# Dilated attention of a hybrid decoder layer: score and value matmuls on the whole array, and one pool of 23 buffers

## The chip, the cores and the metric

The kernel runs on one core of a Trainium2 chip. The metric is the device time of one execution in microseconds (us), as a median over several runs. A core has a matrix engine (PE, with PEld for its weight loads), a vector engine (DVE), a scalar engine (ACT), a general engine (POOL) and a queue engine (SP) that starts most transfers. Each engine works through its own list of instructions in a fixed order and waits, through semaphores, for what its next instruction needs.

## The reference

One decoder layer, in float32, with 512 tokens of width 1024:

```python
y = hybrid_mixer(rms_norm(x, pre_mix_g), w_in, attn_gn_g, ret_gn_g, w_out);   x = x + rms_norm(y, post_mix_g)
y = memory_cross_attn(rms_norm(x, pre_mem_g), mem, ...);                      x = x + rms_norm(y, post_mem_g)
y = swiglu(rms_norm(x, pre_ffn_g), w_gate_up, w_down);                        x = x + rms_norm(y, post_ffn_g)
```

The mixer projects to an attention group (8 heads of 64) and a retention group (4 heads of 128), normalises both and projects the two together. The attention is the part that the change touches: three dilated windows, (128,1), (512,4) and (2048,16), merged by their softmax denominators. For 512 tokens this equals one causal softmax per head, in which a key that lies in several windows counts several times:

```python
outs = [window_attn_by_stride(q, k, v, w, r) for (w, r) in DILATED_PATTERNS]   # o, row max m, denominator l of each
m_all = max(m for _, m, _ in outs)
wts = [l * exp(m - m_all) for _, m, l in outs]
return sum(wt * o for wt, (o, _, _) in zip(wts, outs)) / sum(wts)
```

## The kernel before, in words

**Precision by splitting.** Most products run on the type `fp32r`, which the array takes in one pass. A float32 operand x is written as a high part (x rounded to `fp32r`, on ACT, line 90) and a low part (x minus the high part, on DVE, line 91); this is `split`. A product of two split operands is three matmuls, high by high, high by low and low by high (`mm3`, lines 84 to 86). Plain float32 matmuls are used in the retention, in the transposes and in the attention's values; the trace shows each such product as two records, each transpose as one.

**Weights.** All weights come in 67 chunks of 1 MB, 128 partitions by 2048 values. `load` (from line 101) takes a buffer `raw` for the transfer on SP's queue and a pair `wh`, `wl` for the split. `raw` comes from a pool `rawp` of its own with 2 buffers, the pair from the pool `up` of 20 buffers ("units" of 8 KB per partition), which holds nearly everything else that is large: activations, queries and keys, probabilities. A buffer is reused once its last reader is done.

**Who sets the order.** The program is written in an order that mixes the stages by hand (the attention heads are interleaved with `filler` units: the projections `mk` and `mv` of the memory's keys and values). A scheduler then sets each engine's own list; a change in one stage can therefore move instructions in another.

**The stages.** First comes the projection of the retention's queries and keys (`rqk`, 8 banks of results at a time) while x and the first weights arrive; then `rv`, `rg`, the retention with the attention's projections (`aq`, `ak`, `av`); the attention; the output projection (`o`), the cross attention (`q`, `xs`, `xo`, `o`), and the feed-forward part (`g`, `u`, `dn`).

**The attention, per head.** `att_scores` (from line 431) makes four blocks of scores. The left operand `qk[pr][:, ...]` holds a head's queries with the high part on one half of the partitions and the low part on the other; the right operand holds the keys' high part on both halves, so that the first matmul (line 443) makes qh·kh + ql·kh over 128 rows. The second (line 444) adds qh·kl over 64 rows only: `kl` holds the keys' low part on the head's own half. DVE adds the mask and takes the row maximum (`p`, line 448; then `anm`, line 450), ACT the exponential (line 453). `att_transposes` (from line 457) turns the 10 blocks of probabilities by PE into three banks `ptr`, and copies them out with two ACT copies and one DVE copy (lines 466 to 468) to the unit `pT`. `att_values` (from line 471) multiplies by the values in float32 (line 478): 64 columns of `av` for the left operand, the transposed probabilities as the right one, with the results of a pair of heads in the two halves of one bank `oT`, which ACT copies (line 482). `att_norm` (one per pair) then transposes `ot`, takes the norm in a chain of small DVE operations, and writes `ya`.

Of the kernel before, what the change touches and what calls it, by code (L numbers as in the profile page):

```python
# [11 lines left out]
F32 = mybir.dt.float32  # L12
F32R = mybir.dt.float32r
# [6 lines left out]
P = 128  # L20
D = 1024
# [17 lines left out]
def hybrid_layer(ctx, tc, t, out):  # L39
    nc = tc.nc  # L40
    cp = ctx.enter_context(tc.tile_pool(name="cp", bufs=1))
    up = ctx.enter_context(tc.tile_pool(name="up", bufs=20))
    rawp = ctx.enter_context(tc.tile_pool(name="rawp", bufs=2))
# [6 lines left out]
    def uname(p):  # L50
        cnt[0] += 1
        return f"{p}{cnt[0]}"
# [251 lines left out]
    off = [0, 512, 1024, 896]  # L304
# [64 lines left out]
    qk = [unit("qk", F32R) for _ in range(4)]  # L369
    kl = unit("kl", F32R)  # L370
    av = unit("av")
# [45 lines left out]

    def evict_av(b, ps):
        nc.scalar.mul(av[:, b * 512:(b + 1) * 512], ps, rstd0[:, b:b + 1])

# [7 lines left out]
    def att_scores(h):  # L428
        pr, hh = h // 2, h % 2
        rows = slice(hh * 64, hh * 64 + 64)  # L430
# [7 lines left out]
        for qb in (3, 2, 0, 1):  # L438
            n = (qb + 1) * P
            nn = max(n, 256)  # L440
            c = qk[pr][:, hh * S + qb * P:hh * S + (qb + 1) * P]
            ps = bk[sbank[qb][0]][:, sbank[qb][1]:sbank[qb][1] + nn]
            nc.tensor.matmul(ps, lhsT=c, rhs=qk[pr][:, (2 + hh) * S:(2 + hh) * S + nn], start=True, stop=False)
            nc.tensor.matmul(ps, lhsT=c[rows], rhs=kl[rows, pr * S:pr * S + nn], start=False, stop=True)
# [11 lines left out]

    def att_transposes(h):
        pt = pts.pop(h)
        u = unit("pT")
        bk = [bank("ptr") for _ in range(3)]  # L460
        for kb in (0, 1, 3, 2):
            ps = bk[off[kb] // 512]
            for qb in range(kb, TB):
                o = off[kb] % 512 + (qb - kb) * P
                nc.tensor.transpose(ps[:, o:o + P], pt[:, poff[qb] + kb * P:poff[qb] + (kb + 1) * P], ident)
        nc.scalar.copy(u[:, 0:512], bk[0])
        nc.vector.tensor_copy(u[:, 512:1024], bk[1])
        nc.scalar.copy(u[:, 1024:1280], bk[2][:, :256])
        pTs[h] = u

    def att_values(h):
        pr, hh = h // 2, h % 2
        rows = slice(hh * 64, hh * 64 + 64)
        if hh == 0:
            oTb[pr] = bank("oT")
        u = pTs.pop(h)
        for kb in range(TB):
            nc.tensor.matmul(oTb[pr][rows, kb * P:S], lhsT=av[:, kb * 512 + h * AD:kb * 512 + (h + 1) * AD],
                             rhs=u[:, off[kb]:off[kb] + S - kb * P], start=kb == 0, stop=kb == TB - 1)
        if hh == 1:  # L480
            ot = work("ot")
            nc.scalar.copy(ot, oTb.pop(pr))
            oTb[pr] = ot
# [27 lines left out]
    mem = {}  # L511

    def mem_prepare():
        raw = rawp.tile([P, KT, NM], F32, tag="raw", name=uname("memTr"))
        nc.sync.dma_start(raw, t["memT"])
        m = pair("memT")
        for k in range(KT):
            split(raw[:, k, :], *part(m, k * NM, NM), gT[:, 1, k:k + 1])
        mem["T"] = m
        mem["k"], mem["v"] = pair("kT"), pair("vm")  # L520

    def mem_stats():
        mrow = rawp.tile([P, 2, D], F32, tag="raw", name=uname("mrow"))
# [450 lines left out]
```

## Time and profile before

| what | value |
|---|---|
| median of 3 runs | 829.76 us (829.33 to 831.52) |
| span of the profiled execution, first to last instruction | 828.5 us |
| PE busy | 807.9 us (98%), 4108 matmul records |
| DVE, ACT, POOL busy | 396.6, 305.4, 132.8 us |
| read from memory | 83.11 MB |
| mean granted PE clock | 0.991 |

The profile gives the profiled execution its span but no separate time. The median of the runs is 1.3 us above that span.

How to read it: the page lists busy time by engine; the view of waits says which engine stood idle before which instruction, and for whom; the windows give busy time and PE's granted clock for chosen stretches; the timeline has a row for each instruction or run of equal ones, with its start, its duration and the idle time before it. Matmuls are pipelined, so their durations overlap: the price of one is the distance from its start to the next one's start, not its duration.

### The profile page before, as it was taken

To read this page: it belongs to the slowest core of one execution; us is meant where nothing else is said; L and a number is where in the kernel's file an instruction comes from. 1 tells how busy PE (TensorE), PEld (TensorE's weight loads), DVE (VectorE), ACT (ScalarE), POOL (GpSimd) and SP (SyncE) were. 2 spreads that over 40 slices of the span, in tenths; PEclk is the share of its full clock that TensorE was granted. 3 is DMA by queue.
4 is the path that set the end of the run, shared out by engine and by line. 5 is a ranking of instruction groups with operands and counts; after the bars stand their busy time and mean duration, and the time that the engine had idled before them with its cause. 6 is when DMAs were issued, how large, how long until landed. Compare 5 with 4: busy or idle time off the path is not lost. (4 is left out here: it accounts for less than half of the span.)

```text
span 828.5 us, 10220 instructions
## 1 busy us (share of the span) xinstructions
PE 807.9 (98%) x4108; PEld 675.7 (82%) x4108; DVE 396.6 (48%) x766; ACT 305.4 (37%) x537; POOL 132.8 (16%) x176
## 2 busy tenths in 40 slices
PE   9979999999999999999999899999999999999996
PEld 7768888877777878999988788888888888888884
DVE  5595168764565657758446441405050314222144
ACT  5504333466464733445435232222130305332110
POOL 0161024410110100300036300000000004236000
PEclk9998999999999999999999999999999999999998
DMA  8726212221124440524002340505050322521011
GB/s 305 291 77 236 94 51 87 73 95 52 51 70 175 163 153 0 197 109 153 1 1 102 127 153 1 203 1 203 1 203 1 121 82 74 182 102 51 1 51 51
DMA packets 15519, 85.86 MB, mean 104 GB/s; under 512 B 1904, under 2 KB 1904, under 8 KB 6896
## 3 DMA queue, kind: packets, MB, share of 16 engines
q1 hardware_dynamic: 14752, 84.16, 27.7%
q10 hardware_dynamic: 720, 1.06, 0.3%
q8 instruction: 32, 0.52, 0.3%
q14 instruction: 15, 0.12, 0.0%
HBM read 83.11 MB, written 2.10 MB: 103 GB/s over the span
## 5 line engine op out<-in xcount | busy, mean ns | idle before, releaser
L91 DVE TENSOR_TENSOR wl<-raw,wh 128x1024 fp32r<-128x1024 f32 (+1 forms) x135 | 166.5, 1267 | 102.6 <-ACT wh L90 70.2
L90 ACT CAST wh<-raw 128x1024 fp32r<-128x1024 f32 (+1 forms) x135 | 133.8, 1042 | 95.3 <-DMA raw<-in_w_in 38.1
L820 DVE TENSOR_TENSOR af<-sg,u 128x512 f32<-128x512 f32 x22 | 15.1, 686 | 133.7 <-PE u L86 133.7
L846 POOL TENSOR_TENSOR al<-af,ah 128x512 fp32r<-128x512 f32 x22 | 34.6, 1605 | 257.5 <-ACT ah L845 243.3
L84 PE MATMUL g<-h3h,wh 128*128 128x512 f32 (+1 forms) x192 | 72.1, 375 | 0.0
L84 PE MATMUL u<-h3h,wh 128*128 128x512 f32 (+1 forms) x192 | 71.7, 373 | 0.0
L85 PE MATMUL g<-h3l,wh 128*128 128x512 f32 (+1 forms) x192 | 71.3, 371 | 0.0
L86 PE MATMUL g<-h3h,wl 128*128 128x512 f32 (+1 forms) x192 | 71.3, 371 | 0.0
L85 PE MATMUL u<-h3l,wh 128*128 128x512 f32 (+1 forms) x192 | 71.3, 371 | 0.0
L86 PE MATMUL u<-h3h,wl 128*128 128x512 f32 (+1 forms) x192 | 71.3, 371 | 0.0
L84 PE MATMUL dn<-wh,ah 128*128 128x512 f32 x176 | 68.5, 389 | 0.0
L85 PE MATMUL dn<-wl,ah 128*128 128x512 f32 x176 | 68.5, 389 | 0.0
L86 PE MATMUL dn<-wh,al 128*128 128x512 f32 x176 | 68.5, 389 | 0.0
L817 ACT ACTIVATE sg<-g 128x512 f32<-128x512 f32 x22 | 13.1, 598 | 149.2 <-PE g L86 123.0
L84 PEld LDWEIGHTS g<-h3h,wh 128*128 128x128 f32 x192 | 36.5, 190 | 6.5 <-ACT h3h L90 0.2
L84 PEld LDWEIGHTS u<-h3h,wh 128*128 128x128 f32 x192 | 36.6, 191 | 6.3
L85 PEld LDWEIGHTS g<-h3l,wh 128*128 128x128 f32 x192 | 36.2, 188 | 6.4
L86 PEld LDWEIGHTS g<-h3h,wl 128*128 128x128 f32 x192 | 36.2, 188 | 6.2
L85 PEld LDWEIGHTS u<-h3l,wh 128*128 128x128 f32 x192 | 36.2, 188 | 6.2
L86 PEld LDWEIGHTS u<-h3h,wl 128*128 128x128 f32 x192 | 36.1, 188 | 6.1
L84 PEld LDWEIGHTS dn<-wh,ah 128*128 128x128 f32 x176 | 33.0, 188 | 6.9
L86 PEld LDWEIGHTS dn<-wh,al 128*128 128x128 f32 x176 | 33.0, 188 | 6.9
(267 smaller groups left out, 1752.8 us busy)
## 6 DMA issues: line engine op xcount, KB each, us to landing
raw<-in_w_gu SPq DMA_DIRECT2D x22, 1024.0 KB, 4.8
raw<-in_w_in SPq DMA_DIRECT2D x12, 1024.0 KB, 5.1
raw<-in_w_dn SPq DMA_DIRECT2D x11, 1024.0 KB, 4.7
raw<-in_w_kv SPq DMA_DIRECT2D x8, 1024.0 KB, 4.7
x<-in_x SPq DMA_DIRECT2D x4, 1024.0 KB, 10.2
raw<-in_w_out SPq DMA_DIRECT2D x4, 1024.0 KB, 5.3
raw<-in_w_q SPq DMA_DIRECT2D x4, 1024.0 KB, 5.3
raw<-in_w_o SPq DMA_DIRECT2D x4, 1024.0 KB, 4.7
```

Of the source, the lines that this page charges most:

```text
L84: nc.tensor.matmul(o, lhsT=sh, rhs=mh, start=start, stop=False)
L85: nc.tensor.matmul(o, lhsT=sh, rhs=ml, start=False, stop=False)
L86: nc.tensor.matmul(o, lhsT=sl, rhs=mh, start=False, stop=stop)
L90: nc.scalar.copy(hi, src)
L91: nc.vector.tensor_sub(lo, src, hi.bitcast(F32))
L817: nc.scalar.activation(sg, pg, AF.Silu)
L820: nc.vector.tensor_mul(af[-1][:, (f % 4) * S:(f % 4 + 1) * S], sg, pu)
L846: nc.gpsimd.tensor_sub(lo[:, c], af[i][:, c], hi[:, c].bitcast(F32))
```

## The change

It has four parts.

1. **Scores.** `kl` is now two units. They hold the keys' low part on both halves of the partitions (8 more POOL copies of 64x512), so that the second score matmul uses all 128 rows of the left operand.
2. **Values.** `av` becomes two units of `fp32r`, in which each head's 128 columns are 64 high and 64 low ones (4 more DVE instructions). The transposed probabilities are split into a high and a low unit (`pair("pT")`; three ACT and three DVE instructions per head, where two ACT copies and one DVE copy stood), with two small POOL memsets of zeros. A head's values are 8 `fp32r` matmuls with 128 columns on the left; the upper 64 partitions of the bank hold the part of the high columns, the lower 64 that of the low ones. ACT copies the lower half out (`ol`) and DVE adds the upper half (`ot`), for each head.
3. **Buffers.** The pool `rawp` goes; `raw` comes from the pool `up`, which has 23 buffers in place of 20.
4. A scratch area for transfers is made smaller (`dynamic_dma_scratch_size=1024`).

```diff
-    up = ctx.enter_context(tc.tile_pool(name="up", bufs=20))
-    rawp = ctx.enter_context(tc.tile_pool(name="rawp", bufs=2))
+    up = ctx.enter_context(tc.tile_pool(name="up", bufs=23))
...
-        raw = rawp.tile([P, 2048], F32, tag="raw", name=uname("raw"))
+        raw = unit("raw")
...
-    kl = unit("kl", F32R)
-    av = unit("av")
+    kl = [unit("kl", F32R) for _ in range(2)]
+    av = [unit("av", F32R) for _ in range(2)]
...
+            l = kl[f // 2][:, (f % 2) * 2 * S + i * S:(f % 2) * 2 * S + (i + 1) * S]
             nc.scalar.copy(o[h], v[h])
-            nc.vector.tensor_sub(kl[h, f * S:(f + 1) * S], v[h], o[h].bitcast(F32))
+            nc.vector.tensor_sub(l[h], v[h], o[h].bitcast(F32))
             nc.scalar.copy(o[g], o[h].bitcast(F32))
+            nc.gpsimd.tensor_copy(l[g], l[h].bitcast(F32))
...
     def evict_av(b, ps):
-        nc.scalar.mul(av[:, b * 512:(b + 1) * 512], ps, rstd0[:, b:b + 1])
+        o = av_block(b).rearrange("p (h t d) -> p h t d", h=AH, t=2)
+        v = ps.rearrange("p (h d) -> p h d", h=AH)
+        nc.scalar.mul(o[:, :, 0, :], v, rstd0[:, b:b + 1])
+        nc.vector.scalar_tensor_tensor(o[:, :, 1, :], v, rstd0[:, b:b + 1], o[:, :, 0, :].bitcast(F32),
+                                       op0=ALU.mult, op1=ALU.subtract)
...
-            nc.tensor.matmul(ps, lhsT=c[rows], rhs=kl[rows, pr * S:pr * S + nn], start=False, stop=True)
+            nc.tensor.matmul(ps, lhsT=c, rhs=kl[pr // 2][:, k0:k0 + nn], start=False, stop=True)
...
+    pcol = [(0, 512, 0), (512, 384, P), (1152, 256, 2 * P), (896, 256, 2 * P)]
     def att_transposes(h):
...
-        nc.scalar.copy(u[:, 0:512], bk[0])
-        nc.vector.tensor_copy(u[:, 512:1024], bk[1])
-        nc.scalar.copy(u[:, 1024:1280], bk[2][:, :256])
+        for a in (hi, lo):
+            nc.gpsimd.memset(a[:, 896:1024].bitcast(F32), 0.0)
+        for i, (c0, n) in enumerate(((0, 512), (512, 384), (1024, 384))):
+            split(bk[i][:, :n], hi[:, c0:c0 + n], lo[:, c0:c0 + n])
...
     def att_values(h):
-        for kb in range(TB):
-            nc.tensor.matmul(oTb[pr][rows, kb * P:S], lhsT=av[:, kb * 512 + h * AD:kb * 512 + (h + 1) * AD],
-                             rhs=u[:, off[kb]:off[kb] + S - kb * P], start=kb == 0, stop=kb == TB - 1)
+        for kb, (c0, n, q0) in enumerate(pcol):
+            for i in range(2):
+                nc.tensor.matmul(ps[:, q0:q0 + n], lhsT=av_block(kb, h, 1), rhs=u[i][:, c0:c0 + n],
+                                 start=kb == 0 and i == 0, stop=kb == TB - 1 and i == 1)
...
+        ol = work("ol")
+        nc.scalar.copy(ol[ha], ps[hb])
+        nc.vector.tensor_add(oTb[pr][rows], ps[ha], ol[ha])
```

**How it moves instructions: PE in the attention.** Before, the rows on PE's list from the scores of head 5 to the values of head 3 (`s` scores, `oT` values, `p` probabilities) read:

```order
L443 MATMUL s_1836<-qk_685 128x512
L444 MATMUL s_1836<-kl_687,qk_685 128x512
L443 MATMUL s_1837<-qk_685 128x384
L444 MATMUL s_1837<-kl_687,qk_685 128x384
L443 MATMUL s_1838<-qk_685 128x256
L444 MATMUL s_1838<-kl_687,qk_685 128x256
L443 MATMUL s_1838<-qk_685 128x256
L444 MATMUL s_1838<-kl_687,qk_685 128x256
L478 MATMUL oT_1782<-pT_1787,av_688 64x512
L478 MATMUL oT_1782<-pT_1787,av_688 64x384
L478 MATMUL oT_1782<-pT_1787,av_688 64x256
L478 MATMUL oT_1782<-pT_1787,av_688 64x128
```

Now, after the same scores of head 5, PE's list has (`ptr` are the transposes of head 4):

```order
L490 MATMUL oT_1913<-pTh_1838,av_686 128x512
L475 MATMUL ptr_1927<-ident,p_1765 128x128 x4
L490 MATMUL oT_1913<-pTl_1839,av_686 128x512
L490 MATMUL oT_1913<-pTh_1838,av_686 128x384
L475 MATMUL ptr_1928<-ident,p_1765 128x128 x2
L490 MATMUL oT_1913<-pTl_1839,av_686 128x384
L490 MATMUL oT_1913<-pTh_1838,av_687 128x256
L475 MATMUL ptr_1928<-ident,p_1765 128x128
L475 MATMUL ptr_1929<-ident,p_1765 128x128
L490 MATMUL oT_1913<-pTl_1839,av_687 128x256
L490 MATMUL oT_1913<-pTh_1838,av_687 128x256
L490 MATMUL oT_1913<-pTl_1839,av_687 128x256
```

The values of head 3 are cut up and mixed with the next head's transposes, since each of the value matmuls needs its own piece of `pTl`.

**DVE at the same place.** Before, DVE's list around head 3's one copy (`pT_1787`) reads:

```order
L91 TENSOR_TENSOR wl_1747<-raw_1745,wh_1746 128x1024
L536 TENSOR_TENSOR kf_1778<-mk_1753,mbc 128x256
L467 COPY pT_1787<-ptr_1789 128x512
L536 TENSOR_TENSOR kf_1829<-mk_1804,mbc 128x256
L448 ISA p_1833,amx_1834<-s_1836,lmask 128x512
```

Now it reads:

```order
L496 TENSOR_TENSOR ot_1834<-oT_1825,ol_1835 64x512
L549 TENSOR_TENSOR kf_1886<-mk_1861,mbc 128x256
L90 TENSOR_TENSOR wl_1790<-raw_1788,wh_1789 128x1024 x2
L90 TENSOR_TENSOR pTl_1839<-ptr_1840,pTh_1838 128x512
L90 TENSOR_TENSOR pTl_1839<-ptr_1841,pTh_1838 128x384
L90 TENSOR_TENSOR pTl_1839<-ptr_1842,pTh_1838 128x384
L456 ISA p_1890,amx_1891<-s_1893,lmask 128x512
```

Head 3's low parts (`pTl_1839`), which its values wait for, now stand behind a result of the filler (`kf_1886`) and the split of a weight chunk (`wl_1790`).

**SP at the start.** Before, the transfers behind the last piece of x's transpose (`xraw`) are:

```order
L109 DMA raw_144<-in_w_in 128x2048
L109 DMA raw_156<-in_w_in 128x2048
L161 DMA x_152<-in_x 128x2x1024
L161 DMA x_153<-in_x 128x2x1024
L211 DMA rope_164<-in_rope 128x2048
```

Now they are:

```order
L283 DMA lmask<-in_lmask 128x512
L108 DMA raw_141<-in_w_in 128x2048
L167 DMA g_2349<-in_post_mix_g 128x1024
L167 DMA g_2565<-in_pre_mem_g 128x1024
L160 DMA x_149<-in_x 128x2x1024
L160 DMA x_150<-in_x 128x2x1024
L108 DMA raw_153<-in_w_in 128x2048
L210 DMA rope_161<-in_rope 128x2048
```

The fourth chunk of weights (`raw_156`, now `raw_153`) has moved behind 3.25 MB of other transfers, and on PE's list its first use has moved from the 103rd to the 126th matmul of this projection, while the broadcast of the row norms (`bc`, which DVE's chain of rotations waits for) has moved from the 121st to the 142nd.

**DVE ahead of the feed-forward part.** Before, between the last two normalised blocks `h`:

```order
L626 TENSOR_TENSOR z_4131<-o_4080,g_3470 128x512
L91 TENSOR_TENSOR wl_4190<-raw_4188,wh_4189 128x1024 x2
L91 TENSOR_TENSOR wl_4262<-raw_4260,wh_4261 128x1024 x2
L626 TENSOR_TENSOR z_4131<-o_4081,g_3470 128x512
L630 SCALAR_TENSOR_TENSOR x_2231<-z_4131,pry_4141,x_2231 128x512 x2
L635 SCALAR_TENSOR_TENSOR h_4170<-x_2231,nry_4159,g_3682 128x1024
```

Now:

```order
L639 TENSOR_TENSOR z_4246<-o_4195,g_3585 128x512
L90 TENSOR_TENSOR wl_4305<-raw_4303,wh_4304 128x1024 x2
L639 TENSOR_TENSOR z_4246<-o_4196,g_3585 128x512
L643 SCALAR_TENSOR_TENSOR x_2346<-z_4246,pry_4256,x_2346 128x512 x2
L648 SCALAR_TENSOR_TENSOR h_4285<-x_2346,nry_4274,g_3797 128x1024
```

One chunk's split, where two stood, is ahead of the last block; ACT's list loses the two casts of that chunk at the same place.

More of the change, by code (lines that the diff above doesn't have):

```diff
@@ L429, in att_scores @@
         pr, hh = h // 2, h % 2
-        rows = slice(hh * 64, hh * 64 + 64)
         if hh == 0:
@@ L473, in att_values @@
         rows = slice(hh * 64, hh * 64 + 64)
[L474 to L483 removed]
+        ps = bank("oT")
+        u = pTs.pop(h)
+        for kb, (c0, n, q0) in enumerate(pcol):
+            for i in range(2):
+                nc.tensor.matmul(ps[:, q0:q0 + n], lhsT=av_block(kb, h, 1), rhs=u[i][:, c0:c0 + n],
+                                 start=kb == 0 and i == 0, stop=kb == TB - 1 and i == 1)
+        if hh == 0:
+            oTb[pr] = work("ot")
+        ol = work("ol")
+        nc.scalar.copy(ol[ha], ps[hb])
+        nc.vector.tensor_add(oTb[pr][rows], ps[ha], ol[ha])
     def att_norm(pr):
@@ L513, in mem_prepare @@
     def mem_prepare():
-        raw = rawp.tile([P, KT, NM], F32, tag="raw", name=uname("memTr"))
+        raw = unit("memTr").rearrange("p (k s) -> p k s", k=KT)
         nc.sync.dma_start(raw, t["memT"])
@@ L522, in mem_stats @@
     def mem_stats():
-        mrow = rawp.tile([P, 2, D], F32, tag="raw", name=uname("mrow"))
+        mrow = unit("mrow").rearrange("p (b d) -> p b d", b=2)
         nc.sync.dma_start(mrow, t["mem"].rearrange("(b p) d -> p b d", p=P))
```

20 lines of the change are left out of this document (11 added, 9 removed).

## Prediction

> **What bounds the kernel now.** I read the page's busy times first, then PE's waits, then windows cut at these waits. A window's row gives its ends, its length, the busy time (and instructions) of PE, PEld, DVE, ACT and POOL, PE's granted clock, the DMA share and GB/s.
>
> ```profile
> PE 807.9 (98%) x4108; PEld 675.7 (82%) x4108; DVE 396.6 (48%) x766; ACT 305.4 (37%) x537; POOL 132.8 (16%) x176
> PE rv L85 <- DVE wl L91: 5.2, 1, 5.2
> PE tp L792 <- DVE h L635: 4.0, 1, 4.0
> 56.80:62.10 5.30, 0.14 (x2) 0.01 (x1) 5.18 (x8) 0.00 (x0) 3.58 (x3) 0.75 0.00 0
> 62.10:66.00 3.90, 3.90 (x9) 3.13 (x10) 3.90 (x3) 0.00 (x0) 1.06 (x1) 0.50 0.22 38
> 189.40:264.40 75.00, 74.91 (x422) 54.08 (x420) 44.75 (x133) 41.20 (x102) 6.56 (x8) 1.00 0.20 70
> 469.00:820.70 351.70, 351.61 (x1592) 293.05 (x1592) 104.09 (x129) 88.69 (x119) 34.64 (x22) 1.00 0.24 86
> 820.70:828.50 7.80, 0.00 (x0) 0.00 (x0) 3.81 (x12) 0.69 (x2) 0.00 (x0) 0.71 0.17 67
> ```
>
> PE is the bound nearly everywhere: of the span of 828.5 us it lacks work for two waits worth naming (5.2 and 4.0 us) and a tail of 7.8 us. The attention loop, from 189.4 to 264.4 us, is the stage that the change rewrites: PE is full there, with DVE at 44.75 and ACT at 41.20 of 75.0 us. A microsecond taken from PE there is a microsecond of the kernel, as long as DVE and ACT keep up.
>
> **Scores: what PE saves.** The timeline of PE gives one head's eight score matmuls between two runs of the filler:
>
> ```profile
> 237.97 0.28 PE L85 MATMUL mk<-memTl,wh 128*128 128x256 f32 x1
> 238.09 0.28 PE L86 MATMUL mk<-memTh,wl 128*128 128x256 f32 x1
> 240.01 0.39 PE L443 MATMUL s<-qk 128*128 128x512 f32 x1
> 240.33 0.50 PE L444 MATMUL s<-kl,qk 64*128 64x512 f32 x1
> 240.76 0.44 PE L443 MATMUL s<-qk 128*128 128x384 f32 x1
> 241.13 0.45 PE L444 MATMUL s<-kl,qk 64*128 64x384 f32 x1
> 241.50 0.38 PE L443 MATMUL s<-qk 128*128 128x256 f32 x1
> 242.76 0.39 PE L84 MATMUL mk<-memTh,wh 128*128 128x256 f32 x1
> 260.38 0.40 PE L86 MATMUL mv<-wh,memTl 128*128 128x512 f32 x1
> 260.61 0.39 PE L84 MATMUL mv<-wh,memTh 128*128 128x512 f32 x1
> ```
>
> Start to start, a full-array matmul of 256 columns costs 0.12 us and one of 512 costs 0.23; for 384 I take 0.175, halfway. In the scores the same sizes cost more: 512 columns 0.32 on all rows and 0.43 on 64 rows, 384 columns 0.37 and 0.37, and the head's eight take 240.01 to 242.76, 2.75 us. What sets them apart from the filler is the alternation of 128 and 64 rows, which ends with the change. The eight are then two of each: 2 x 0.23 + 2 x 0.175 + 4 x 0.12 = 1.29 us. Eight heads save 8 x 1.46 = 11.7 us. If the price lies not in the alternation but in these operands, nothing is saved: 0 is the lower bound. The Trainium skill, "TensorEngine Tiling (Array Packing)", section "Key Properties", says that changing the tiling mode drains the engine; by that rule every one of these gaps is a drain that goes, and the trace's gaps agree.
>
> **Values.** One head's float32 matmuls, eight records, from their start to the next instruction's:
>
> ```profile
> 262.06 2.37 PE L478 MATMUL oT<-pT,av 128*64 128x512 f32 x8
> 264.36 0.66 PE L300 MATMUL yt<-ident,rg 128*128 128x128 f32 x4
> ```
>
> That is 2.30 us. The new eight have 512, 384, 256 and 256 columns twice, so 1.29 us as above; eight heads save 8 x 1.01 = 8.1 us. If they ran at the scores' present spacing (2.64 us by the rows above), they would lose 2.7 us; I take the filler's, whose operands and array they share. PE saves 19.8 us in all, 6 x 1.46 + 8.1 = 16.9 of it inside the window of 75.0 us, which would shrink to 58.1.
>
> **What DVE and ACT pay there.** The groups by form in that window:
>
> ```profile
> L91 DVE TENSOR_TENSOR wl<-raw,wh 128x1024 fp32r<-128x1024 f32 x10 | 11.9, 1219 | 1.4 <-ACT wh L90 1.4
> L467 DVE COPY pT<-ptr 128x512 f32<-128x512 f32 x8 | 5.5, 688 | 8.6 <-PE ptr L465 8.6
> L536 DVE TENSOR_TENSOR kf<-mk,mbc 128x256 f32<-128x256 f32 x8 | 3.4, 424 | 12.1 <-PE mk L86 12.0
> L448 DVE CUSTOM_DVE_ANT_0 p<-s,lmask 128x512 f32<-128x512 f32 (+3 forms) x24 | 11.0, 488 | 2.8 <-PE s L444 2.7
> L503 DVE TENSOR_TENSOR ya<-otr,ary 128x512 f32<-128x512 f32 x3 | 2.1, 691 | 0.2
> L145 DVE TENSOR_TENSOR arw<-ary 128x8 f32<-128x8 f32 x9 | 1.5, 167 | 0.2
> L466 ACT COPY pT<-ptr 128x512 f32<-128x512 f32 x8 | 4.7, 584 | 11.7 <-PE ptr L465 11.6
> L468 ACT COPY pT<-ptr 128x256 f32<-128x256 f32 x8 | 3.0, 370 | 0.2
> 46.63 0.69 DVE L246 TENSOR_TENSOR t<-rqk,rope 64x512 f32<-64x512 f32 x1
> ```
>
> Per head DVE loses a copy (0.69) and gains three low parts, 1.79 us (0.69 for 512 columns and 0.55 for each of two with 384, halfway between the copy's 0.69 and `kf`'s 0.42 for 256), and the 64x512 addition (0.69, as the `t` row): +1.79 us. Eight heads: 14.3, so 44.75 becomes 59.1 us in a window that PE would leave after 58.1. ACT gains two casts of 384 for one copy of 256 (about 0.5 each against 0.37) and `ol` in each head for half an `ot` (0.59 against 0.29): +0.93 a head, 41.20 becomes 48.6, with room.
>
> So DVE catches up with PE, and the question is what PE waits. I went along both orders from head 2's transposes to head 6's values. PE: 62 transposes at 0.11 (the next rows), 4 scores and 5 values of 1.29, 7 fillers of 24 x 0.12: 38.6 us.
>
> ```profile
> 235.99 1.31 PE L465 MATMUL ptr<-ident,p 128*128 128x128 f32 x10
> 237.05 0.36 PE L84 MATMUL mk<-memTh,wh 128*128 128x256 f32 x1
> ```
>
> DVE: 5 x 1.79 of low parts, 5 x 0.69 of additions, 4 x 1.83 of `p` (11.0 us for six heads), 7 x 0.42 of `kf`, four chunks of `wl` (8 x 1.22), three norm chains of 3.6 (two large steps as `ya`, 13 small ones as `arw`) and four of `anm`, as small: 44 us. DVE falls 5.4 us behind. A little of that may be late without harm (the last norm, a chunk for later matmuls), and some is added where DVE itself stands waiting, for `kf_1886` above all, ahead of the low parts that head 3's values need. I take 5 us of waiting for PE. Bounds: 0 if the mixing of transposes with values hides it; 11.4 if DVE can be kept only 85% busy (59.1 / 0.85 - 58.1).
>
> **The rest.** The eight POOL copies for `kl`, the memsets and the four DVE instructions for `av` lie off PE's path. The copies run beside the projections of the keys, where PE has 24 x 0.23 = 5.5 us of work per step and a POOL operation of twice their size takes 1.46 us:
>
> ```profile
> L411 POOL TENSOR_TENSOR t<-t,rope 128x512 f32<-128x512 f32 x6 | 8.7, 1457 | 14.1 <-DVE t L409 14.0
> ```
>
> Without that cover the last four copies, 6 us at most, would hold up the scores of the later heads.
>
> At the start, the fourth weight chunk now follows 3.25 MB of other transfers, and the chain of rotations on DVE that ends PE's wait of 5.2 us begins later:
>
> ```profile
> 23.63 2.00 ACT L90 CAST wh<-raw 128x1024 fp32r<-128x1024 f32 x2 [1.64 <-DMA raw<-in_w_in]
> 35.84 2.00 ACT L90 CAST wh<-raw 128x1024 fp32r<-128x1024 f32 x2 [0.45 <-DMA raw<-in_w_in]
> 33.65 0.46 PE L176 MATMUL bc<-diag,ones 128*128 128x128 f32 x2 [0.30 <-DVE diag L175]
> 36.76 0.69 DVE L177 COPY rbc<-bc 128x512 f32<-128x512 f32 x1 [0.58 <-PE bc L176]
> ```
>
> Between 23.6 and 35.8 us five megabytes landed (x, `rope`, two chunks), so 3.25 MB cost about 8 us, and the chunk lands near 31 instead of 23.6. PE asked for it 18 matmuls ahead of the broadcast, near 29 us, and now asks 23 later, near 34: no stall. The broadcast stands 21 matmuls later, 0.23 each, so `rbc` and the end of PE's wait move by 4.4 to 4.8 us; but PE has 23 more matmuls (5.2 us) ahead of that wait. Net 0, from -1 to +4 if the transfers are slower.
>
> The second wait, ahead of the feed-forward part:
>
> ```profile
> 450.09 3.88 ACT L90 CAST wh<-raw 128x1024 fp32r<-128x1024 f32 x4
> 453.87 0.59 ACT L624 ACTIVATE junk<-o 128x512 bf16<-128x512 f32 x1
> 467.72 1.28 DVE L635 SCALAR_TENSOR_TENSOR h<-x,nry,g 128x1024 f32<-128x1024 f32 x1 [4.56 <-POOL nry L141]
> ```
>
> The squares of the last block stood behind four casts on ACT; one chunk's two casts (1.94 us) are gone from there, so the chain to `h` ends 1.9 us earlier. I take -2 us, between -4 (the wait gone) and 0.
>
> As all chunks now share the pool, most `raw` transfers wait for a unit that PE frees. Load and split take 4.7 + 2.1 + 2.4 = 9.2 us:
>
> ```profile
> raw<-in_w_kv SPq DMA_DIRECT2D x8, 1024.0 KB, 4.7
> ```
>
> By the order, with PE's matmuls priced as above, the tightest chunk of the attention (`raw_2288`) has its last unit freed 10 us of PE work before its first use, the others 12 or more: no cost, but little to spare.
>
> **Sum.** 828.5 - 19.8 + 5 + 0 - 2 = 811.7 us of span. The runs' median lies 1.3 us above the profiled span; with that, 813 us.
>
> **Rivals.**
>
> *DVE paces the attention.* If it is busy only 85% of the time, PE waits 11.4 us: 828.5 - 19.8 + 11.4 - 2 + 1.3 = 819.4. For it: its 59.1 us stand in a strict order with results of PE between them. Against: the waits of DVE today show idle time that is slack, not bubbles. It gets worse if PE's gaps grow long: after the wait of 5.2 us the clock row shows 0.50 for 3.9 us, 2 us lost; my gaps are 1 to 2 us each. The Trainium skill, "TensorE: Matmul & The Clock Gate", section "Why this matters for your kernels", puts the danger at idle gaps above about 3 us; one wait here (5.2 us) agrees, the other (4.0 us) was followed by the window from 469 us at clock 1.00.
>
> *The scores don't get cheaper.* If the spacing belongs to the operands, or if 64 rows were the cheap form, 11.7 us stay: with PE slower, DVE's lag goes too, 828.5 - 8.1 - 2 + 1.3 = 819.7; if the new values share that spacing it is 830.5. Against: 512 columns on 64 rows take 0.43 here, a full-array matmul 0.23. The Trainium skill speaks for it in "TensorEngine Tiling (Array Packing)", section "Theoretical Speedup": up to twofold for a contraction of 64 or less, when tiles run side by side; here each 64-row matmul stands between full ones, and its row bears no gain out.
>
> *Slower: the shared pool starves the weights.* A chunk whose unit PE frees less than 9.2 us before use stalls PE, and DVE's list stands still behind its `wl`. The kernel turns slower when such stalls pass 829.8 - 813 = 16.8 us; 1 us at each of the 33 feed-forward chunks gives 846, half of it on top of the first rival 836. Against: there each chunk has 48 x 0.23 = 10.9 us of PE work, and by the order its units are free 20 us or more ahead.
>
> **Chances.** Forecast 0.64 (808 to 817); DVE paces 0.18 (817 to 823); scores not cheaper 0.09 (820 to 831); starved and slower 0.05 (833 to 850); better than forecast, with no wait in the attention, 0.04 (805 to 808). The range 806 to 821 leaves out the starved case, nearly all of the third and the outer ends of the second and the last, 0.2 in all. A measurement of this kernel tells 0.3%, 2.5 us, from no change. Faster 0.93, the same 0.03, slower 0.04.
>
> **What would show it.** Right: the eight scores of a head span 1.3 us, the eight values 1.3 us of matmuls with gaps for `pTl` on DVE among PE's waits, 3 to 8 us in sum; DVE near full in the window; the wait on `h` at 2 us. Wrong: scores still at 0.3 us each; PE waiting for `wl` or `wh` with a transfer behind it; PE's clock below 1.00 in the attention.

## The result and the profile after

The changed kernel takes 840.08 us (median of 4 runs, 838.71 to 842.38) against 829.61 us before (4 runs): a ratio of 1.0126, 95% interval 1.0107 to 1.0145. It is slower by 10.5 us, where 813 us were forecast and 806 to 821 us given as the range. The profiled execution spans 836.9 us, 8.4 us more than before. One execution of e5 below, its profiled one, ran at half the matmul rate throughout (span 1597.0 us); it is left out, and that kernel was profiled again as e8.

The line of busy times on the page of the changed kernel:

```profile
PE 794.9 (95%) x4108; PEld 680.1 (81%) x4108; DVE 409.9 (49%) x794; ACT 310.4 (37%) x549; POOL 133.5 (16%) x200
```

and PE's longest waits in it (engine, line, what it waited for, us in total, times, longest):

```profile
PE rv L84 <- DVE wl L90: 5.7, 1, 5.7
PE q L85 <- DVE wl L90: 4.8, 4, 2.4
PE s L451 <- DVE av L426: 4.7, 1, 4.7
PE otr L503 <- DVE ot L496: 3.4, 2, 2.0
PE ptr L475 <- DVE pTl L90: 2.8, 1, 2.8
PE tp L805 <- DVE h L648: 2.6, 1, 2.6
PE mk L83 <- DVE ot L496: 1.7, 1, 1.7
PE q L83 <- ACT wh L89: 1.7, 1, 1.7
```

PE is busy 13 us less and yet ends later: two waits worth naming have become eight. Where the clock is full, a head's matmuls came down as forecast. The timeline of PE, one head's first score, first value and what follows:

```profile
207.85 0.40 PE L451 MATMUL s<-qk 128*128 128x512 f32 x1
...
209.14 0.40 PE L490 MATMUL oT<-pTh,av 128*128 128x512 f32 x1
...
210.43 1.25 PE L475 MATMUL ptr<-ident,p 128*128 128x128 f32 x10
```

Eight scores take 207.85 to 209.14, eight values 209.14 to 210.43: 1.29 us each, to the hundredth what the prediction worked out.

To see where the time went I cut both executions at the same PE instructions: the first scores, the first transposes of probabilities, the first `yt`, the first `q` and the first `xs` (windows as in the prediction: ends, length, busy PE, PEld, DVE, ACT, POOL, PE's clock). Before, from the first scores on, and the query projection:

```profile
172.35:189.46 17.11, 16.71 (x66) 11.76 (x64) 11.34 (x29) 11.94 (x25) 0.41 (x1) 1.00 0.19 62
189.46:264.36 74.90, 74.81 (x421) 54.04 (x419) 44.75 (x133) 41.14 (x102) 6.56 (x8) 1.00 0.20 70
331.50:357.37 25.87, 25.53 (x214) 25.29 (x213) 19.61 (x38) 11.65 (x24) 8.33 (x19) 1.00 0.57 204
```

The same three stages after:

```profile
174.78:195.51 20.73, 16.06 (x66) 13.09 (x64) 15.61 (x34) 14.38 (x28) 3.26 (x7) 0.84 0.15 51
195.51:263.63 68.12, 59.61 (x422) 55.85 (x421) 53.08 (x155) 44.94 (x112) 8.03 (x22) 0.97 0.31 109
332.64:366.32 33.68, 26.82 (x213) 25.57 (x212) 21.24 (x36) 13.98 (x26) 6.84 (x19) 1.00 0.34 126
```

The stage of the first two heads' scores was to lose 2 x 1.46 = 2.9 us and gained 3.6: 6.5 us are missing. The attention loop was to lose 6 x 1.46 + 8.1 = 16.9 and lost 6.8: 10.1 us missing. The query projection, in which the change edits nothing, gained 7.8. Up to the first scores the kernel is 2.4 us later, between loop and query projection 1.9, and behind it 0.5 are won back. In sum 6.5 + 10.1 + 7.8 + 2.4 + 1.9 - 0.5 = 28.2 us lost, less the 19.8 saved: 8.4.

In the query projection the transfers can be seen to come late. SP's timeline, the transfers of `w_q` and of the gain vectors; before:

```profile
292.92 41.89 SPq L109 DMA_DIRECT2D raw<-in_w_q  x4
...
344.25 0.33 SPq L168 DMA_DIRECT2D g<-in_post_mem_g  x1
```

and after:

```profile
291.76 22.02 SPq L108 DMA_DIRECT2D raw<-in_w_q  x2
340.18 0.33 SPq L167 DMA_DIRECT2D g<-in_post_mem_g  x1
340.60 0.38 SPq L108 DMA_DIRECT2D raw<-in_w_q  x1
348.46 0.33 SPq L167 DMA_DIRECT2D g<-in_pre_ffn_g  x1
348.84 0.43 SPq L108 DMA_DIRECT2D raw<-in_w_q  x1
```

What SP's queue waited longest for between 300 and 352 us in the changed kernel:

```profile
SPq L167 <- DVE z L639: 26.3, 1, 26.3
SPq L108 <- PE o L84: 21.3, 1, 21.3
```

Before, the four `w_q` transfers start at 292.9, 299.2, 331.9 and 334.5 us, the first two while the output projection still runs, into the two buffers that hold nothing but landing transfers. After, the second waits 21.3 us for a unit that PE's output projection holds, and the third and fourth stand in SP's order behind two gain vectors, of which the first waits 26.3 us for DVE's last `z`. PE asks for the first of these weights at 332.64. Which of this PE waits for, e6 below tells.

### The profile page after: what moved, and what is told of

It reads as the page before. It is cut to its first block, busy times and chain, and to the rows that moved or that the text cites. A ratio compares the mean times of both kernels' runs of the same rounds, so it can differ in the third digit from the quotient of the medians.

```text
span 836.9 us, 10294 instructions
## 1 busy us (share of the span) xinstructions
PE 794.9 (95%) x4108; PEld 680.1 (81%) x4108; DVE 409.9 (49%) x794; ACT 310.4 (37%) x549; POOL 133.5 (16%) x200
## 4 chain that ended last, share of the span: by engine, by line
PE 52%; DVE 4%; POOL 3%; issue 2%; DMA 1%; ACT 1%; DVEq 0%; SPq 0%; POOLq 0%; ACTq 0%
PE dn L84 5%; PE dn L83 5%; PE dn L85 5%; PE g L84 5%; PE g L85 5%; PE u L84 5%; PE u L85 5%; PE g L83 5%; PE u L83 4%; PE o L83 1%; PE o L85 1%; PE o L84 1%; PE q L85 1%; PE q L83 1%; PE q L84 1%
## 5 line engine op out<-in xcount | busy, mean ns | idle before, releaser
L90 DVE TENSOR_TENSOR wl<-raw,wh 128x1024 fp32r<-128x1024 f32 (+1 forms) x135 | 163.6, 1250 | 94.9 <-ACT wh L89 83.9
L859 POOL TENSOR_TENSOR al<-af,ah 128x512 fp32r<-128x512 f32 x22 | 31.2, 1452 | 255.3 <-ACT ah L858 248.8
L85 PE MATMUL q<-hhh,wl 128*128 128x256 f32 x128 | 35.9, 287 | 4.8 <-DVE wl L90 4.8
```

The costliest lines, as they stand in the source:

```text
L85: nc.tensor.matmul(o, lhsT=sl, rhs=mh, start=False, stop=stop)
L90: nc.vector.tensor_sub(lo, src, hi.bitcast(F32))
L859: nc.gpsimd.tensor_sub(lo[:, c], af[i][:, c], hi[:, c].bitcast(F32))
```

## Experiments

Two theories stood at the start. Theory 1: the shared pool makes the transfers late or puts their splits in other places. Theory 2: the work added on DVE and ACT holds PE up, and the pool has no part.

**e1: the changed kernel with raw buffers of its own.**

```diff
-    up = ctx.enter_context(tc.tile_pool(name="up", bufs=23))
+    up = ctx.enter_context(tc.tile_pool(name="up", bufs=21))
+    rawp = ctx.enter_context(tc.tile_pool(name="rawp", bufs=2))
...
-        raw = unit("raw")
+        raw = rawp.tile([P, 2048], F32, tag="raw", name=uname("raw"))
```

(`memTr` and `mrow` likewise.)

> The changed kernel with the raw weight chunks back in two buffers of their own (21 units and 2 raw buffers, the same 23 x 8 KB). Theory 1, the shared pool: weight transfers and their splits came late or in another order, which cost about 2.4 us up to the first scores, 6.5 us up to the first transposes, part of the 10 us in the attention loop and 7.8 us in the query projection. Then this kernel keeps PE's 19.8 us and loses only what DVE holds up in the attention: 813 to 822 us. Theory 2, the extra work of DVE and ACT (low parts, additions) makes the waits and the pool has no part in it: 832 to 842 us, as the changed kernel.

819.85 us, ratio to before 0.9874 (0.9859 to 0.9889): 20.2 us faster than the changed kernel with the same memory and the same arithmetic. The smaller scratch area stayed, so it isn't what costs the time. Windows of the same three stages, and the largest wait of PE that before did not have:

```profile
172.90:193.13 20.23, 16.65 (x65) 13.36 (x64) 16.03 (x36) 16.93 (x31) 3.86 (x7) 0.83 0.28 104
193.13:253.08 59.95, 57.61 (x421) 54.38 (x420) 54.14 (x155) 46.25 (x113) 8.67 (x23) 1.00 0.28 91
320.59:346.45 25.86, 25.52 (x213) 25.27 (x212) 19.55 (x38) 11.78 (x24) 8.38 (x19) 1.00 0.55 204
```

```profile
PE s L452 <- DVE av L427: 2.8, 1, 2.8
```

The query projection is back at its 25.9 us. The attention loop takes 59.95, 15.0 us less than before, of 16.9 forecast, with DVE at 54.14 of 59.95 us: 90% busy, and PE still nearly full. What remains missing, 6 us, lies in the first stage, where only 0.5 us came back. By the same cuts the pool's share of the span, 18.6 us, is 8.2 in the attention loop, 7.8 in the query projection, 1.9 ahead of the first scores, 1.5 between loop and query projection and 0.5 in the first stage, less 1.3 behind.

**e2: the kernel before with the shared pool alone.**

```diff
-    up = ctx.enter_context(tc.tile_pool(name="up", bufs=20))
-    rawp = ctx.enter_context(tc.tile_pool(name="rawp", bufs=2))
+    up = ctx.enter_context(tc.tile_pool(name="up", bufs=23))
...
-        raw = rawp.tile([P, 2048], F32, tag="raw", name=uname("raw"))
+        raw = unit("raw")
```

(`memTr`, `mrow` and the smaller scratch as in the change.)

> The kernel before with one edit alone: all raw chunks drawn from one pool of 23 units. No matmul changes. Theory 1 (the pool): slower by 8 to 18 us, 838 to 848 us, with PE waiting on weight splits of the query projection. Theory 2 (DVE's extra work): no change, 828 to 832 us.

842.26 us, ratio 1.0151 (1.0134 to 1.0167): slower than the whole change. Its query projection and its waits there:

```profile
336.18:369.98 33.80, 29.00 (x213) 28.15 (x212) 21.25 (x36) 13.99 (x26) 6.87 (x19) 0.90 0.38 126
```

```profile
PE q L85 <- DVE wl L90: 4.5, 3, 2.8
```

33.80 against 25.87 us: 7.9 of its 11.3 us of span are here, 2.2 before the first `aq`. Its attention loop takes 74.97 us, as before (74.90): there the pool costs only together with the other edits. That this is because they hold three or four units more (`kl`, `av`, and the low halves of `pT`) is likely, but no run shows it. Theory 2 as the main cause is out.

**e3: the full-array scores alone**, on the kernel before with 21 units, 2 raw buffers and the smaller scratch.

```diff
-            nc.tensor.matmul(ps, lhsT=c[rows], rhs=kl[rows, pr * S:pr * S + nn], start=False, stop=True)
+            nc.tensor.matmul(ps, lhsT=c, rhs=kl[pr // 2][:, k0:k0 + nn], start=False, stop=True)
```

(and the change's edits of `kl` in `split_k`.)

> The kernel before, 21 units and 2 raw buffers, with the full-array scores alone (both halves of the low part of k). Theory 1: the 11.7 us of PE come through, less a little where PE now meets DVE: 818 to 821 us. Theory 2, attention is paced by DVE and ACT as soon as PE gets faster: 824 to 830 us.

824.24 us, ratio 0.9931 (0.9916 to 0.9945). First scores to first transposes, and the loop:

```profile
172.80:192.83 20.03, 16.93 (x65) 13.51 (x64) 14.85 (x34) 17.75 (x35) 3.66 (x5) 0.83 0.28 106
192.83:259.00 66.17, 66.08 (x421) 52.65 (x419) 42.90 (x130) 39.37 (x95) 6.61 (x8) 1.00 0.22 79
```

In the loop six heads give 74.90 - 66.17 = 8.7 us, all of 6 x 1.46 = 8.8. In the stage ahead two heads were to give 2.9, and it is 2.9 longer. So the missing 6 us come with the scores alone, without any added work on DVE for the values. The time lies in theory 2's range, but not for its reason: the loop isn't paced by DVE.

Where they go can be added up. PE's work in this stage takes 13.9 us at full clock (the window of e13):

```profile
171.66:188.35 16.69, 13.88 (x65) 11.38 (x64) 13.65 (x25) 14.90 (x28) 3.32 (x7) 1.00 0.34 126
```

e3's stage has 16.93 us of busy PE, so 3.0 us go to the half clock, and 3.1 to waits (1.8 and 1.3 us, both for ACT's eviction of `av`), where before waited 0.4. In e1 it is 2.8 and 3.6. ACT's second eviction of `av`, before and in e3:

```profile
183.12 0.69 ACT L419 ACTIVATE av<-av,r0y 128x512 f32<-128x512 f32 x1
183.60 0.69 ACT L421 ACTIVATE av<-av,r0y 128x512 f32<-128x512 f32 x1
```

Both stand 10.8 us behind the first scores, and the first evictions 8.8 us (181.13 and 181.60): they follow the rotation of the last key, which the change doesn't shorten. PE gets there earlier and waits for what it saved; the half clock behind the wait costs as much again.

**e4: the split values alone**: e1 with the scores of before.

```diff
-            nc.tensor.matmul(ps, lhsT=c, rhs=kl[pr // 2][:, k0:k0 + nn], start=False, stop=True)
+            nc.tensor.matmul(ps, lhsT=c[rows], rhs=kl[rows, pr * S:pr * S + nn], start=False, stop=True)
```

(and `kl` and `split_k` as before.)

> The kernel before, 21 units and 2 raw buffers, with the split values alone (low part of the transposed probabilities, V as 64 high and 64 low columns). PE saves 8.1 us, DVE does 14.3 us more. Theory 1: 822 to 826 us, since DVE has room while the scores are still slow. Theory 2 (DVE's work paces): 830 to 838 us.

829.80 us, ratio 0.9995 (0.9983 to 1.0007), just below theory 2's range. The loop takes 70.60 us and loses 4.3 of the 8.1 forecast; the stage ahead takes 19.17 and gains 2.1. By themselves the split values bring nothing; with the scores, on e3, they bring 824.24 - 819.85 = 4.4 us.

**e6: the gain vectors behind the `w_q` chunks**, in the changed kernel with its shared pool.

```diff
-    def load_gain(name):
+    def load_gain(name, behind=None):
         g = wk.tile([P, D], F32, tag="g", name=uname("g"), bufs=2)
+        if behind is not None:
+            nc.scalar.copy(g[:, :1], behind[0][:, 2047:2048].bitcast(F32))
...
-    g3 = load_gain("post_mem_g")
+    g3 = load_gain("post_mem_g", wq[3])
```

(`g4` likewise.)

> The changed kernel with its shared pool, where the two gain vectors loaded in the query projection wait for the last w_q chunk's high part (a one-column copy on ACT into each gain's buffer), which puts their transfers behind the w_q chunks in SP's order. Theory 1a (the two late w_q chunks, issued at 340.6 and 348.8 us, stood in SP's queue behind a gain transfer that waits for DVE's last z): PE's waits of 7.3 us in the query projection go, 831 to 835 us. Rival 1b (the units of those chunks are themselves free only then): 838 to 842 us, as the changed kernel.

837.46 us, ratio to before 1.0079 (1.0058 to 1.0100): 2.6 us better than the changed kernel, between the two expectations. SP's timeline, the query projection's window, and PE's longest wait there:

```profile
294.28 39.86 SPq L108 DMA_DIRECT2D raw<-in_w_q  x4
```

```profile
335.21:366.14 30.93, 26.28 (x213) 25.43 (x212) 21.23 (x36) 14.24 (x28) 6.83 (x19) 1.00 0.28 99
```

```profile
PE q L85 <- DVE wl L90: 4.3, 3, 2.4
```

All four transfers are now issued ahead of the gains, by 334.1 us (before: 334.5), and 2.8 of the 7.8 us are gone: that much is theory 1a's. Rival 1b falls, since the last two chunks' units are free by then, not only at 340.6 and 348.8. The other 5.1 us are mostly waits for `wl`, but not for transfers. ACT's casts of the first two chunks, before and then in e6:

```profile
327.02 3.93 ACT L90 CAST wh<-raw 128x1024 fp32r<-128x1024 f32 x4
330.68 2.01 ACT L89 CAST wh<-raw 128x1024 fp32r<-128x1024 f32 x2
338.50 1.98 ACT L89 CAST wh<-raw 128x1024 fp32r<-128x1024 f32 x2
```

The second chunk was issued at 316.0 us and took 4.8 to land, so it lay there for 17 us ahead of its casts. In ACT's and DVE's order its split now stands behind a residual's squares, `x` and norm, and PE waits 2.4 us for it in e6 as in the changed kernel. Neither theory named this, and why the order comes out so with the shared pool isn't shown; with the buffers apart (e1) the query projection has its old length.

**e7: e1 without the low part on DVE.** The three subtractions per head and the low part's unit are left out, and the high part is multiplied twice, so PE's work is unchanged and the low bits of the probabilities are lost.

```diff
-            split(bk[i][:, :n], hi[:, c0:c0 + n], lo[:, c0:c0 + n])
-        pTs[h] = hi, lo
+            nc.scalar.copy(hi[:, c0:c0 + n], bk[i][:, :n])
+        pTs[h] = hi, hi
```

> The kernel of e1 without the low part of the transposed probabilities: DVE's three subtractions per head (1.79 us) are left out, and the second matmul of each pair takes the high part again, so PE's work is the same and the product loses the probabilities' low bits. If DVE's added work holds PE up in the attention by 5 to 11 us as the prediction's forecast and first rival had it, 809 to 815 us; if it holds PE up by no more than the 2 us that e1's attention loop leaves, 817 to 820 us.

818.09 us, ratio to before 0.9855 (0.9839 to 0.9870), 1.8 us under e1. Its loop:

```profile
192.97:251.45 58.48, 57.42 (x421) 54.39 (x420) 44.12 (x134) 46.16 (x113) 8.33 (x15) 1.00 0.29 96
```

Ten microseconds less on DVE (44.12 against 54.14) shorten the loop by 1.5. That is the price of DVE's low parts, hardly more than the spread of the runs, and the first stage (20.00 us) doesn't feel them.

**e5, e8, e9, e10: where do the missing 6 us of the first stage come from?** In e1, ACT's four casts and DVE's four low parts of the first two key chunks stand ahead of the evictions of `av`, for whose bank PE waits. In e5 and e8 (one kernel) both chunks are loaded behind the values' projection; in e9 and e10 only the second, behind the memory's own splits or ahead of them.

```diff
-                ws[:] = [take("w_in", c0, 1), take("w_in", c0 + 1, 2)]
+                ws[:] = [take("w_in", c0, 1), take("w_in", c0 + 1, 0 if c0 == 12 else 2)]
...
     avs[3]()
+    ahead("w_kv", 0)
     mem_prepare()
+    ahead("w_kv", 1)
```

> The kernel of e1 (raw chunks in two buffers of their own) with the first two chunks of the memory's keys loaded behind the values' projection in the program, not ahead of it, so that their four casts on ACT (4.2 us) and four low parts on DVE (4.9 us) no longer stand ahead of the evictions of av in those engines' orders. Theory 1 (e1 loses 6 us between its first scores and its first transposes because PE's second head of scores waits for a bank that such an eviction frees, 2.8 + 0.8 us, and then runs 4 us at half clock): 813 to 816 us, no wait of PE for av. Rival: the chain of rotations and casts of the last key ends too late by itself, and the splits only fill its pauses: 819 to 821 us, as e1.

> The kernel of e5 once more, whose times (823 to 825 us) missed both expectations and whose one profiled execution cannot be read. Theory 1c: the wait for av's evictions is gone, as expected, but the moved splits now stand on ACT and DVE with those of the memory ahead of the first head's transposed probabilities, and PE waits there by 8 to 10 us. Rival: the wait for av is still there (2 us or more), since the chain of the last key decides it. 822 to 826 us in either case.

> The kernel of e1 with only the second of the two early key chunks loaded later: behind the memory's own transfer and splits. Two casts (2.1 us) and two low parts (2.4 us) leave ACT's and DVE's orders ahead of av's evictions; the first mk product waits for nothing new, since it needs the first chunk alone. Theory 1 (the order ahead of av's evictions costs e1 its 6 us): the wait of 2.8 + 0.8 us falls under 1.5 us, the half clock behind it goes, 814 to 817 us. Theory 1c (the moved splits cost as much in the first head's transposes): 819 to 823 us.

> The same with the second key chunk loaded behind the values' projection but ahead of the memory's own transfer and splits. Theory 1: 814 to 817 us as e9. Theory 1c: slower than e9 by 1 to 4 us, since the memory's splits, and the first head's transposed probabilities behind them, come later.

e5 took 824.9 us (ratio 0.9928, 0.9907 to 0.9949), e8 824.2, e9 822.28 (0.9915, 0.9895 to 0.9936), e10 822.63 (0.9905, 0.9891 to 0.9920): all above e1. PE's waits in e8:

```profile
PE ptr L476 <- DVE pTl L91: 4.9, 1, 4.9
...
PE s L452 <- DVE av L427: 1.5, 1, 1.5
```

The wait for `av` shrinks in e8, and a longer one stands at the first heads' transposes. In e9 and e10 it is 2.7 us, as in e1, and a new one of 3.5 and 2.4 us stands at the transposes. Theory 1 in this form falls: what is moved out of the first stage is paid for in the next. Theory 1c is right in that; but e10, which it had 1 to 4 us above e9, is level with it.

**e11, e12: those splits off DVE, and off ACT too.** The kernel of e1; the low parts of the two chunks, and in e12 the casts too, go to POOL.

```diff
+            elif key in (("w_kv", 0), ("w_kv", 1)):
+                nc.scalar.copy(w[0][:, c], raw[:, c])
+                nc.gpsimd.tensor_sub(w[1][:, c], raw[:, c], w[0][:, c].bitcast(F32))
             else:
                 split(raw[:, c], w[0][:, c], w[1][:, c])
```

(e12: `nc.gpsimd.tensor_copy` for the cast.)

> The kernel of e1 with the low parts of the first two key chunks computed on POOL, not DVE: 4.9 us leave DVE between the first scores and the second head's transposes, where e1 has DVE busy 21.0 and ACT 21.9 of 25.2 us. Theory 1d (that stretch is bound by what ACT and DVE have to do in it, wherever it stands): 815 to 818 us, more on ACT than on DVE being left. Rival (the chain of the last key, the evictions and the exponentials decides by its length): 819 to 822 us.

> The same with the casts of these two chunks on POOL too: 4.2 us leave ACT as well. Theory 1d: 813 to 817 us, PE's wait for av gone or under 1 us and no new wait at the first transposes. Rival (length of the chain): 819 to 822 us. If POOL is too slow for them, PE waits for wl at the first mk product and the time is above e1.

821.20 us (0.9896, 0.9878 to 0.9914) and 820.00 us (0.9873, 0.9856 to 0.9891): no gain on e1. PE's wait for `av` is 5.9 us in e11 and 3.4 us in e12. DVE got no faster by what was taken from it: over first stage and loop it is busy 71.6 us in e11 and 69.4 in e12, against 70.2 in e1. Its timeline in e12:

```profile
177.00 2.07 DVE L415 TENSOR_TENSOR t<-t,rope 128x512 f32<-128x512 f32 x1
```

and POOL's at the same time:

```profile
176.12 2.40 POOL L118 TENSOR_TENSOR wl<-raw,wh 128x1024 fp32r<-128x1024 f32 x1
```

The product `t` of the last key takes 2.07 us beside POOL's `wl`, three times its 0.69 us in e1. In e11, beside 11 us of such subtractions, the sum `t` takes 2.78 us (0.69 in e1) and the last key's two low parts 4.83 (1.39 in e1); they lengthen the very chain that the evictions of `av` follow. So these two don't decide between the theories as cleanly as was meant: POOL's work is paid on DVE.

**e13, e14: the evictions of `av` first on ACT.** The kernel of e1, and in e14 that of e9, with the last key's casts held behind the first two evictions by a one-column copy that they then write over.

```diff
+            if f == 3:
+                nc.scalar.copy(o[h][:, :1], av[0][h, 1024:1025].bitcast(F32))
             nc.scalar.copy(o[h], v[h])
...
     avs[0]()
-    flush()
     avs[1]()
     att_scores(0)
+    flush()
     avs[2]()
```

> The kernel of e1 with the last key's casts forced behind the first two evictions of av on ACT: a one-column copy out of av into each of the two places that these casts then write over, and the same step moved behind the first scores in the program. Theory 1e (ACT stands idle, or does splits, while av's results wait in their banks, because the order has the last key's casts ahead of them): the wait of 2.8 + 0.8 us falls to 1 us or less and the half clock behind it goes, 814 to 817 us. Rival (DVE's four low parts of the key chunks stand ahead of av's low part in any case, and the stretch as a whole has no room): 818 to 821 us.

> The same with the second key chunk loaded behind the memory's splits, as in e9: nothing but the first chunk's splits stands ahead of av's evictions on ACT and DVE. Theory 1e: no wait for av, 813 to 817 us. Rival (what leaves this place comes back as a wait at the first head's transposes, as in e8 to e10): 819 to 823 us.

819.45 us (0.9870, 0.9855 to 0.9885) and 820.68 us (0.9890, 0.9870 to 0.9910): e1's time again, the rivals' expectation. PE's new wait in e13 is at the transposes:

```profile
PE s L454 <- DVE av L429: 2.8, 1, 2.8
PE ptr L478 <- ACT p L464: 2.0, 2, 1.9
```

In e14 the wait for `av` at the scores is 0.5 us, and PE waits 3.1 us for its last low part at the transposes.

From the first scores to the first `yt`, e1 takes 80.2 us (20.23 + 59.95), and the windows cut at the same instructions give 84.6 in e8, 83.3 in e9 and in e10, 82.1 in e11, 82.8 in e12, 81.7 in e13 and 80.9 in e14. Seven kernels with the same work in other places, and none is below e1, though e14's 0.7 us more is within the spread of single runs.

## Why the prediction was wrong

By its own steps, in its order:

- *What bounds the kernel.* Right for before. One reading failed: the 4.0 us wait ahead of the feed-forward part was said to be followed by full clock, from a window of 351.7 us. The clock was half for 3.4 us; a window of 3 us behind the wait shows it:

```profile
469.30:472.30 3.00, 3.00 (x13) 2.68 (x13) 2.20 (x4) 1.80 (x3) 0.00 (x0) 0.50 0.00 0
```

- *Scores* (-11.7) and *values* (-8.1). Right as PE's own work: 1.29 us a head each. In time, the loop's part of the scores came in full (8.7 of 8.8 us, e3). The first two heads' part (2.9) never came, and the stage grew by as much again: PE waits there for `av`, and the clock halves.
- *What DVE and ACT pay* (+5, bounds 0 to 11.4). e1's loop takes 59.95 us where 58.1 were worked out for PE alone, so 1.9 us in place of 5. Without DVE's low parts the time is 1.8 us less (e7), and DVE fills e1's loop to 90%. The rival by which 85% is DVE's limit fell: it goes to 90% in e1 with 2.3 us of PE idle.
- *The rest*: the start was priced at 0 within -1 to +4 and cost 2.4 us up to the first scores. The wait for `h` did shrink, from 4.0 to 2.6 us, but from the first `g` to the first `dn` nothing came of it (248.5 us after, 248.3 before): the half clock behind it lasts 6.8 us now, 3.4 before. The shorter wait goes with the pool (2.7 us in e2, 4.0 in e1).
- *The shared pool: 0.* This is the step that failed. The pool costs 20.2 us in this kernel (840.08 against e1's 819.85) and 12 us alone (e2), most of it in the attention loop (8.2) and in the query projection (7.8). The prediction set "unit freed by PE" against "first use" in PE's work, named the attention as the tightest place, and looked neither at the query projection nor at where a chunk's split then stands (only its third rival named DVE standing still behind `wl`). Three things were missed. First, the two raw buffers let two chunks land a whole stage ahead; with one pool a chunk lands only when its unit is free, and in the query projection that is 14 us later for the second chunk (issued at 313.45 us, as its row ends at 291.76 + 22.02 and one issue takes 0.33, against 299.17); this chunk still landed ahead of its split, so PE did not wait for its transfer as such. Second, SP's queue is in order: a transfer that waits for its unit holds up all behind it, and the new order put two gains ahead of two chunks (2.8 us, e6). In the attention the memory's transfer waited 30.8 us for PE (4.2 us before), and the next chunk another 20.5; SP's queue between 150 and 232 us of the changed kernel:

```profile
SPq L528 <- PE s L452: 30.8, 1, 30.8
SPq L108 <- PE s L452: 20.5, 1, 20.5
```

  Third, the splits stand elsewhere, and other work stands behind them. DVE's timeline at the first head's low parts:

```profile
197.70 3.25 DVE L93 SCALAR_TENSOR_TENSOR memTl<-memTr,gT,memTh 128x256 fp32r<-128x256 f32 x8
200.87 1.61 DVE L90 TENSOR_TENSOR pTl<-ptr,pTh 128x512 fp32r<-128x512 f32 x3
```

  The memory's eight low parts, 3.25 us, stand directly ahead of `pTl`, for which PE waited 2.8 us at `ptr`. PE's other three long waits in the loop (1.5, 1.7 and 2.0 us) each end behind a chunk's split too; the last of them, for `ot`:

```profile
250.74 2.36 DVE L90 TENSOR_TENSOR wl<-raw,wh 128x1024 fp32r<-128x1024 f32 x2 [3.53 <-ACT wh L89]
253.13 0.68 DVE L496 TENSOR_TENSOR ot<-oT,ol 64x512 f32<-64x512 f32 x1
```

  e1 differs from the changed kernel in the pool alone, and its loop is 8.2 us shorter: 6.2 less of PE idle, and 2.0 less of busy PE, as its clock stays full. Why the shared pool puts the splits there is not shown.
- *The signs.* Of those that were to show the prediction wrong, two came: PE waiting for `wh` and `wl` with a transfer behind it (2.8 us for the last two `w_q` chunks), and a clock below 1.00 in the attention (0.97, and 0.84 in the stage ahead).
- *Rivals.* The third, that the shared pool starves the weights and makes the kernel slower, was the right one, with 0.05. It was argued down in the feed-forward part, where it is indeed harmless (e2: from the first `g` on, 0.7 us less than before); the place was the query projection and the attention.

With the pool's 20.2 us taken off, 819.85 us stand against 813 forecast. In spans it is 818.3 against 811.7: the first stage 6.0 us more, the loop 3.1 less, nothing of the 2 us on `h`, and 1.7 over the rest. That 819.85 falls into the stated range, and next to the first rival's 819.4, is luck: DVE's waits, which that rival puts at 11.4 us, are 1.9. The prediction didn't see the first stage because it moved PE's saving of all eight heads through one sum. From its first scores to its first values before takes 22.2 us (172.35 to 194.53), of which the change takes 2.9 from PE; the variants take 23.4 (e13) to 28.0 us (e8). That this stretch is not paced by PE is shown by e1, e3 and e8 to e14. In e1 and e3 the first thing that holds PE up is the eviction of `av` behind the last key's rotation, and the half clock doubles the loss. Which link would set the stretch without that (the casts, the exponentials, the first transposed probabilities) stays open: three places were changed, and the time moved between them. That the new POOL copies for `kl` hold it up isn't borne out: in this stretch of e1 and e3 no wait of PE is for POOL.

## What to carry to other kernels

In this kernel the landing buffers' own pool was not spare memory: it decoupled the time of a transfer from the time at which the last stage's operands are freed, and giving two buffers to a common pool of 23 cost more (12 us alone) than the matmul work that the memory paid for saved in its best form (10 us, e1). Before such a merge, go through every stage, list when each chunk's transfer is issued on the queue and what stands ahead of it in that queue, not only when its unit comes free; then see, in each engine's order, what its split stands behind and whose work stands behind it. And a saving on PE counted here only in the stages in which PE is what ends last: sum it stage by stage.

## What the runs showed of the hardware

- DVE ran slower beside POOL. Its 128x512 product took 2.07 us while POOL ran a 128x1024 subtraction (2.40 us, e12), against 0.69 us without it (e1), and the two 64x512 subtractions of the last key took 4.83 us in e11 against 1.39; moving 4.9 us of DVE's work to POOL gave nothing. The Trainium skill, "GPSIMD Engine Reference", section "1. Specifications", names contention with DVE instructions that read two tensors from SBUF, as this product does; the row agrees and puts the price at a factor of three.
- The clock halved behind waits shorter than the prediction had reckoned with, and the length of one wait didn't decide it. In the attention of the changed kernel the clock is 0.50 for 6.8 us around the wait of 4.7 us and for 3.4 us behind that of 2.8; in e1 it is 0.50 for 6.8 us from the end of the wait of 2.8 us on. In e4 the first stage has no wait longer than 0.8 us, and the clock is 0.50 there for 3.4 us, beginning 2.4 us behind it. But in e13 PE waited 2.8 us for `av` and the stage stayed at 1.00 (the half clock came 12 us later, behind a wait of 1.9), and the wait of 2.4 us in the changed kernel's query projection was followed by none. By the Trainium skill, "TensorE: Matmul & The Clock Gate", section "Why this matters for your kernels", gaps above about 3 us are the danger; these runs put it lower, down to 0.8 us, and at no fixed length. In such a stretch PE's matmuls take twice their time, so 3.4 us of it cost up to 1.7 us and 6.8 us up to 3.4, besides the wait.
